# Dense expert weights built in steps of eight tokens, with the weighted one-hots on ScalarE

## Chip, cores and metric

One core of a Trainium2 chip. The metric is the device time of one execution in microseconds (us); the kernel before is given as the median of three runs.

## What is computed

A transformer block on 512 tokens (plus 16 meta tokens) of width 1024: a gated linear recurrence, an attention branch, and then a layer of 16,384 small experts, of which each token takes 128 (16 of each of 8 heads). The part that matters here is that layer:

```python
idx = jnp.take_along_axis(cidx, sel, axis=-1)
g = jax.nn.softmax(ts, axis=-1)
act = jax.nn.gelu(jnp.einsum('chkd,cd->chk', u[idx], xt))
coef = (g * act.astype(jnp.float32)).astype(xt.dtype)
return jnp.einsum('chk,chkd->cd', coef, v[idx])
```

`u` and `v` are the two expert tables. `idx` and `g` are, for each token, the 128 chosen experts and their softmax weights.

## The kernel before

The tokens are four chunks of 128. For three of them the experts are not gathered: the whole tables are multiplied, in 128 blocks of 128 experts. For a block, a first product gives gelu(x . u) as [expert, token] (function `first_dense`, float32r parts, lines 181 to 183 and the activation at line 820), this is multiplied by a dense table of softmax weights that is zero for experts that were not chosen, and a second product with v gives the output. The fourth chunk gathers its rows by index.

The dense table of a chunk is made by `scatter` (line 843), once for each of the three chunks, and goes to DRAM (`gd`) in four pieces of 32 tokens. An expert index is split into its block (upper bits) and its place in the block (lower bits). For each token, one 128x128 product adds up its 128 choices: the left operand `hot` is the one-hot of the place, the right operand `wj` the one-hot of the block times the softmax weight, and the outcome is [place, block].

The work goes in groups of four tokens, 96 groups in all:

- line 868, VectorE: `hb`, the one-hots of the blocks of four tokens in bf16, laid out [choice, block, token], the token innermost;
- line 870, VectorE: `hot`, the one-hots of the places, float32, [choice, token, place];
- lines 873 to 877: the weighted one-hot `wj` of each token, 128 elements, read out of `hb` in steps of four bf16 elements (8 bytes). ScalarE makes three of four (line 875, its scale is a column of `gt_`), VectorE the fourth (line 877);
- line 878, TensorE: four products in float32, into one PSUM bank of the ring `mm2` (three banks). Each appears as two matmul records, so 768 records for 384 products;
- line 879, ScalarE: the eviction of the bank's 512 columns into the staging tile `stg`, [place, block, token] with 32 tokens. It reads PSUM in order and writes one float32 every 32, that is, every 128 bytes.

`stg` has one buffer. After eight groups it is sent to DRAM by SyncE's queue (line 881). `hb`, `hot` and `wj` have two buffers each, in a pool `sp_` that is closed after the stage.

Three generators run in step (`interleave`, line 890): `scatter` of one chunk, `choose` of the next chunk (VectorE for the most part), and `first_ahead` (line 830), first products of expert blocks ahead of time, with their weight loads (line 166) and splits on ScalarE (line 155) and VectorE (line 156). Within an engine the order is not the program's: a scheduler orders the instructions by a model of their times, and each engine then runs its queue in that order. Only in the stretch after (`dense`, line 958, from 966 us on) is VectorE held to the program's order. There `stage` (line 939) loads the dense table and splits v into `vh` and `vl`, two buffers each of 4 KB a partition, in a pool `vp` that is open from before the dense-weight stage. 40 blocks of the first product are made before that stretch, however long the stage takes.

Of the kernel before, what the change touches and what calls it, by code (L numbers as in the profile page):

```python
# [8 lines left out]
F32 = mybir.dt.float32  # L9
# [12 lines left out]
NK = 8            # 128-row pieces of D_MODEL  # L22
NM = 16           # meta tokens
# [4 lines left out]
NH = 16           # attention heads  # L28
SCALE = 96.0 ** -0.5
PH = 8            # PEER heads  # L30
TOPK = 16
NS = PH * TOPK    # chosen experts of a token
NCAND = 50        # pairs (a, b) of ranks with (a + 1) * (b + 1) <= 16
NEG = -3.0e38
BIG = 1.0e30
# The pair of rank k (from 0) has (a + 1) * (b + 1) <= k + 1: blocks (a0, na, b0, nb) of pairs, by the
# group of four ranks that they can first have.
# [5 lines left out]
CO = (3, 0, 2, 1)    # chunks of queries of a pair of heads: the two sizes of the probabilities in turn  # L43
NJ = 128          # blocks of 128 experts
LAG = 41          # blocks that the first product runs ahead of the second
TS = 32           # tokens of a piece of the dense weights
JG = 4            # blocks of a load of the dense weights
# How the experts of a chunk are computed. Chunk 0: rows of both tables fetched by index.
# Chunks 1 to 3: products with both whole tables, times the dense softmax weights.
NDC = 3  # L50
ORD = (mybir.EngineType.DVE,)
SCA = 3           # tokens of four that ScalarE scales
LT = 2            # blocks of the first product between the two phases
GE = 6            # steps by which the fetches of rows end early
GA = ((0, 2), (2, 5))          # gate tiles that are computed between those of the recurrent branch
# [3 lines left out]
DT = NDC * P      # tokens of the dense chunks  # L59

# columns of the packed per-feature vectors
# [7 lines left out]
class in_order:  # L69
    """Keeps the instructions of the given engines that are traced within in the order of the program."""  # L70
# [22 lines left out]
def now(gen):  # L93
    """Runs a generator through; what it returns."""
    while True:
        try:
            next(gen)
        except StopIteration as e:
            return e.value
# [7 lines left out]
def interleave(*gens):  # L107
    """Runs generators in step, by the share of each that is done."""
    items = [[g, n, 0] for g, n in gens if n]
    while items:  # L110
        it = min(items, key=lambda i: i[2] / i[1])
        try:
            it[2] += next(it[0]) or 1
        except StopIteration:
            items.remove(it)
# [3 lines left out]
def hybrid_block_kernel(ctx: ExitStack, tc, hT, x, win, wkr, vecs, wgate, wrnn, watt, wuq, wukv, wout,  # L119
# [38 lines left out]
    wn = [0, 0, None]         # pieces, more buffers of the parts and their pool  # L158

    def wload(src, n, name):  # L160
        """A weight tile of n columns: its two float32r parts, in pieces of 512 columns."""
# [28 lines left out]
    # K' of a head: 64 rows without position, then the rotated rows twice  # L190
# [12 lines left out]
    def bcast_rms(sq, pieces, dim, dst, name):  # L203
        """dst = sqrt(mean of squares + eps) of every token (column), on all partitions."""
        for t0, n in pieces:
            o = mm1(f"{name}_ss{t0}")
            for k, q in enumerate(sq):
                TE.matmul(o[:, :n], onesP, q[:, t0:t0 + n], start=k == 0, stop=k == len(sq) - 1)
            A.activation(dst[:, t0:t0 + n], o[:, :n], AF.Sqrt, bias=eps_t, scale=1.0 / dim)

    # The projections take h * g; their outcomes are scaled by the token's 1/rms.
# [6 lines left out]
    def proj_tile(wi, full, name, src=None, m=P, w=None):  # L218
        """One tile of w_in: PSUM pieces (first token, tokens, psum); full: with the meta tokens."""
# [22 lines left out]
    def two(tags, name):  # L242
        """Eight [P, T] pieces in the space of two tiles."""
# [56 lines left out]
    def latent_norms():  # L300
        """The rotated key rows of all buffers, the normed latent of keys and values, the queries' scales."""
# [17 lines left out]
    # 8 * log_sigmoid(lambda) = 8 * (min(l, 0) - log1p(exp(-|l|)));  # L319
    # log1p(z) = 2 * atanh(y), y = z / (2 + z) <= 1/3  # L320
# [11 lines left out]
    for d in (13, 11, 9, 7, 5, 3, 1):  # L332
# [8 lines left out]
          for k in range(NK)]                              # recurrent output  # L341
    def sig_tile(wi, name):
        """Sigmoid of a tile of w_in."""
# [10 lines left out]
    def out_rnn(m):  # L354
        """A tile of the recurrent branch's gated outcome."""
# [11 lines left out]
    for hb in range(NK // HB):  # L367
# [53 lines left out]
        # 1 - a^2 = -tanh(log a) * (1 + a^2)  # L421
# [39 lines left out]
    def fm_pieces(pl, name):  # L461
        """A feature-major operand: the two parts of each 128-feature piece."""
# [5 lines left out]
    # the meta tokens in one product: rows hi, hi, lo of the values by hi, lo, hi of the probabilities  # L468
# [8 lines left out]
    def att_pair(pr):  # L477
        """Keys and values of a pair of heads."""
# [19 lines left out]
        # values of the tokens of each chunk  # L498
# [9 lines left out]
    def att_query(pr, j, pair):  # L508
        """Queries of a head."""
# [9 lines left out]
    def att_scores(st):  # L519
# [7 lines left out]
        for (k0, n), sp in zip(pieces, sps):  # L527
            d0 = nk - P - k0         # the diagonal block
# [20 lines left out]
    def att_turn(st):  # L549
        """Probabilities with the keys on the partitions, in parts; those of both heads side by side."""  # L550
# [21 lines left out]
    def att_out(st):  # L572
        """[feature of the pair, query of each head]: a head's own half of the features counts."""
# [54 lines left out]
    xdp = pool(ctx, "xd", "right")  # L628
    mx_ = pool(mixx, "mix")
    # normed input of the experts, feature-major: the dense chunks, then chunk 0  # L630
# [32 lines left out]
    def dense_products(j, o, w=None):  # L663
        """x . u of expert block j for the dense chunks: [expert, token]."""
# [7 lines left out]
    def mixing():  # L672
        """Attention output, gated sum of the branches, residual, second norm."""
# [50 lines left out]
    def key_scores():  # L724
        """Scores of the expert keys, the 16 best of each half."""
# [31 lines left out]
    def choose(i, c):  # L757
        """The 16 best pairs of each head, their indices and softmax weights."""
# [64 lines left out]
    def first_dense(j, o, w=None):  # L823
        """gelu(x . u) of expert block j for the dense chunks: [expert, token]."""
# [15 lines left out]
    iota4 = sp_.tile([P, P, 4], BF16, name="iota4")  # L840
    V.tensor_copy(iota4, iota.unsqueeze(2).to_broadcast([P, P, 4]))

    def scatter(gi, val, ef):
        """Dense [expert in block, block, token] weights of a chunk, to DRAM: one-hot products of each token."""
# [17 lines left out]
        for q in range(P // TS):  # L862
            stg = sp_.tile([P, NJ, TS], F32, tag="stg", bufs=1, name=f"stg{gi}_{q}")
            for t4 in range(0, TS, 4):
                o = mm2(f"sc{gi}_{q}_{t4}")
                t0 = q * TS + t4
                hb = sp_.tile([P, P, 4], BF16, tag="hb", bufs=2, name=f"hb{gi}_{t0}")
                V.tensor_tensor(hb, iota4, blk[:, t0:t0 + 4].unsqueeze(1).to_broadcast([P, P, 4]), op=OP.is_equal)
                hot = sp_.tile([P, 4, P], F32, tag="hot", bufs=2, name=f"hot{gi}_{t0}")
                V.tensor_tensor(hot, iota.unsqueeze(1).to_broadcast([P, 4, P]),  # L870
                                it[:, t0:t0 + 4].unsqueeze(2).to_broadcast([P, 4, P]), op=OP.is_equal)
                wj = sp_.tile([P, 4, P], F32, tag="wj", bufs=2, name=f"wj{gi}_{t0}")
                for u in range(4):
                    if u < SCA:
                        A.activation(wj[:, u, :], hb[:, :, u], AF.Copy, scale=gt_[:, t0 + u:t0 + u + 1])  # L875
                    else:
                        V.tensor_scalar(wj[:, u, :], hb[:, :, u], gt_[:, t0 + u:t0 + u + 1], None, op0=OP.mult)
                    TE.matmul(o[:, u * P:(u + 1) * P], hot[:, u, :], wj[:, u, :], start=True, stop=True)  # L878
                A.copy(stg[:, :, t4:t4 + 4].rearrange("p j t -> p t j"), o.rearrange("p (t j) -> p t j", t=4))  # L879
                yield  # L880
            nc.sync.dma_start(gd[gi, q], stg)
# [24 lines left out]
    def first_by_index(c):  # L906
        """coef = softmax weight * gelu(u[idx] . x) of the chosen experts."""
# [31 lines left out]
    def stage(j):  # L939
        """Operands of step j: the parts of u of block j + LAG, of v and of the coefficients of block j."""  # L940
# [61 lines left out]
def _consts():  # L1002
    """Constants that depend on the shapes alone."""
# [22 lines left out]
def _layout(i):  # L1026
# [7 lines left out]
    def tiles(w):                      # [K, N] -> [N / 128][128 of K][K / 128 * 128 of N]  # L1034
# [17 lines left out]
    uq = np.concatenate([uq, uq[..., 80:96], uq[..., 64:80]], -1)               # 3, p, h, 128  # L1052
# [30 lines left out]
```

## Time and profile before

| | |
|---|---|
| runs | 1882.66, 1877.91, 1879.43 us; median 1879.43 |
| span of the profiled execution | 1876.3 us (the page gives no other time for it) |
| TensorE matmul busy | 1821.0 us, 97% |
| VectorE busy | 1470.3 us, 78% |
| ScalarE busy | 981.4 us, 52% |
| GpSimd busy | 356.4 us, 19% |
| dense-weight stage | 719 to 966 us, 247 us |

The shares are means over stages that have different limits; the stage of the change is some 13% of the span. A group's mean duration is longer than the distance of two such instructions that follow each other, since they overlap in part: the busy time of a group counts an overlap once.

### The profile page before, as it was taken

How to read it: one execution, taken by the hardware profiler on the slowest of the kernel's cores; microseconds unless marked ns; L12 is line 12 of the kernel's file. 1: busy time of each engine (PE TensorE's matmuls, PEld its weight loads, DVE VectorE, ACT ScalarE, POOL GpSimd, SP SyncE). 2: the span in 40 equal slices, each digit the busy share in tenths (PEclk: the TensorE clock that was granted, in tenths of full speed). 3: DMA queues.
4: the chain of work that ended last, by engine and by line, in shares of the span. 5: the costliest groups of instructions: out<-in, count | busy, mean ns of one | idle time of the engine just before them, and what ended most of it. 6: DMA issues, size and time to landing. Idle time of an engine off the chain costs nothing.

```text
span 1876.3 us, 28456 instructions
## 1 busy us (share of the span) xinstructions
PE 1821.0 (97%) x9731; PEld 1600.0 (85%) x9731; DVE 1470.3 (78%) x3280; ACT 981.4 (52%) x1915; POOL 356.4 (19%) x295
## 2 busy tenths in 40 slices
PE   8999999999999999999999999999999999999997
PEld 7888778877788888888899999998999999998886
DVE  7787677777546999898858788787887888887775
ACT  5778576766334337999963333333333333333343
POOL 0100000000100000000014344344444444443310
PEclk9999999999999999999999999999999999999999
DMA  5333212112733223454569999989998899988764
GB/s 162 92 101 104 74 54 66 62 55 85 241 113 129 85 85 130 144 194 158 189 225 348 321 318 340 326 300 322 324 334 313 304 331 321 343 309 280 266 223 152
DMA packets 181602, 390.34 MB, mean 208 GB/s; under 512 B 16593, under 2 KB 68305, under 8 KB 179921
## 3 DMA queue, kind: packets, MB, share of 16 engines
q1 hardware_dynamic: 141632, 245.97, 38.9%
q0 software_dynamic: 39536, 142.00, 21.8%
q8 instruction: 76, 1.25, 0.3%
q14 instruction: 70, 0.57, 0.1%
q10 hardware_dynamic: 288, 0.56, 0.1%
HBM read 353.44 MB, written 34.08 MB: 207 GB/s over the span
## 4 chain that ended last, share of the span: by engine, by line
PE 73%; ACT 10%; DMA 6%; DVE 6%; issue 3%; POOL 0%; DVEq 0%; ACTq 0%; SPq 0%; POOLq 0%
PE y L183 8%; PE y L182 8%; PE y L181 8%; PE a L183 7%; PE a L182 7%; PE a L181 7%; ACT stg L879 4%; PE q L181 2%; PE q L182 2%; PE wgr_ps L228 2%; PE q L183 2%; PE wga_ps L228 2%; PE wgn_ps L228 2%; PE sc L878 2%; ACT wj L875 2%
## 5 line engine op out<-in xcount | busy, mean ns | idle before, releaser
L183 PE MATMUL a<-xdh,ut_l 128*128 128x384 f32 x1024 | 346.3, 338 | 4.3 <-DVE ut_l L156 4.3
L181 PE MATMUL a<-xdh,ut_h 128*128 128x384 f32 x1024 | 348.1, 340 | 0.7 <-ACT act L820 0.5
L182 PE MATMUL a<-xdl,ut_h 128*128 128x384 f32 x1024 | 345.7, 338 | 0.3 <-DVE xdl L156 0.3
L155 ACT CAST ut_h<-ut_w 128x512 fp32r<-128x512 f32 x256 | 159.2, 622 | 330.3 <-DMA ut_w<-in_peer_uT_dram 281.7
L183 PE MATMUL y<-vh,cl 128*128 128x512 f32 x768 | 300.6, 391 | 0.0
L182 PE MATMUL y<-vl,ch 128*128 128x512 f32 x768 | 300.3, 391 | 0.0
L181 PE MATMUL y<-vh,ch 128*128 128x512 f32 x768 | 299.0, 389 | 1.3 <-ACT ch L155 1.3
L902 POOL DMA_INDIRECT u<-in_peer_u_dram,eidx x128 | 162.7, 1271 | 682.9 <-DMA gt<-gd 458.5
L902 POOL DMA_INDIRECT v<-in_peer_v_dram,eidx x128 | 175.2, 1369 | 262.6 <-DVE acc L922 233.6
L156 DVE TENSOR_TENSOR ut_l<-ut_w,ut_h 128x512 fp32r<-128x512 f32 x256 | 170.5, 686 | 52.2 <-ACT ut_h L155 51.7
L183 PEld LDWEIGHTS a<-xdh,ut_l 128*128 128x128 f32 x1024 | 193.0, 188 | 5.2 <-DVE ut_l L156 5.0
L181 PEld LDWEIGHTS a<-xdh,ut_h 128*128 128x128 f32 x1024 | 193.0, 188 | 4.7 <-ACT act L820 0.9
L182 PEld LDWEIGHTS a<-xdl,ut_h 128*128 128x128 f32 x1024 | 192.9, 188 | 3.9 <-DVE xdl L156 0.5
L156 DVE TENSOR_TENSOR vl<-vr,vh 128x1024 fp32r<-128x1024 f32 x128 | 157.6, 1232 | 40.6 <-ACT vh L155 40.4
L155 ACT CAST ch<-gt 128x384 fp32r<-128x384 f32 x128 | 65.7, 513 | 233.8 <-DVE gt L952 228.8
L922 DVE SCALAR_TENSOR_TENSOR acc<-v,coef,acc 128x1024 f32<-128x1024 f32 x128 | 164.1, 1282 | 11.3 <-DMA v<-in_peer_v_dram,eidx 9.2
L183 PEld LDWEIGHTS y<-vh,cl 128*128 128x128 f32 x768 | 144.1, 188 | 30.6 <-DVE cl L156 0.3
L181 PEld LDWEIGHTS y<-vh,ch 128*128 128x128 f32 x768 | 144.2, 188 | 30.0 <-ACT ch L155 2.1
L182 PEld LDWEIGHTS y<-vl,ch 128*128 128x128 f32 x768 | 144.1, 188 | 28.4
L913 DVE SCALAR_TENSOR_TENSOR jk<-u,xn 128x1024 bf16<-128x1024 f32 x128 | 156.5, 1222 | 14.7 <-DMA u<-in_peer_u_dram,eidx 12.2
L155 ACT CAST vh<-vr 128x1024 fp32r<-128x1024 f32 x128 | 133.7, 1045 | 31.7 <-PE y L183 26.9
L156 DVE TENSOR_TENSOR cl<-gt,ch 128x384 fp32r<-128x384 f32 x128 | 71.5, 559 | 80.9 <-ACT ch L155 80.9
(349 smaller groups left out, 3569.2 us busy)
## 6 DMA issues: line engine op xcount, KB each, us to landing
ut_w<-in_peer_uT_dram SPq DMA_DIRECT2D x256, 256.0 KB, 6.2
vr<-in_peer_v_dram SPq DMA_DIRECT2D x128, 512.0 KB, 6.4
gd<-stg SPq DMA_DIRECT2D x12, 2048.0 KB, 7.3
gt<-gd SPq DMA_DIRECT2D x96, 256.0 KB, 6.9
wq_w<-in_wq_dram SPq DMA_DIRECT2D x32, 256.0 KB, 2.7
wxr_w<-in_win_dram SPq DMA_DIRECT2D x16, 256.0 KB, 2.7
wgr_w<-in_win_dram SPq DMA_DIRECT2D x16, 256.0 KB, 2.8
wga_w<-in_win_dram SPq DMA_DIRECT2D x16, 256.0 KB, 2.6
```

Of the source, the lines that this page charges most:

```text
L155: A.copy(dst_hi, src)
L156: V.tensor_sub(dst_lo, src, r32(dst_hi))
L181: TE.matmul(o, lh, rh, start=first, stop=False)
L182: TE.matmul(o, lh, rl, start=False, stop=False)
L183: TE.matmul(o, ll, rh, start=False, stop=last)
L228: TE.matmul(o[:m, :n], lhs, rhs[:, k, t0:t0 + n], start=k == 0 and i == 0, stop=k == NK - 1 and i == 2)
L875: A.activation(wj[:, u, :], hb[:, :, u], AF.Copy, scale=gt_[:, t0 + u:t0 + u + 1])
L878: TE.matmul(o[:, u * P:(u + 1) * P], hot[:, u, :], wj[:, u, :], start=True, stop=True)
L879: A.copy(stg[:, :, t4:t4 + 4].rearrange("p j t -> p t j"), o.rearrange("p (t j) -> p t j", t=4))
L902: G.indirect_dma_start(out=t, out_offset=None, in_=src, in_offset=bass.IndirectOffsetOnAxis(ap=eidx[:, s:s + 1], axis=0))
L913: V.scalar_tensor_tensor(jk, t, 1.0, xn2, op0=OP.mult, op1=OP.mult, accum_out=coef[:, s:s + 1])
L922: V.scalar_tensor_tensor(acc, t, coef[:, s:s + 1], acc, op0=OP.mult, op1=OP.add)
```

## The change

A step is eight tokens (`SG`) in place of four, 48 steps in all.

- `hb` is [choice, block, 8 tokens], made by one VectorE instruction of 1024 elements, and `hot` one of 1024 elements. There are 48 of each in place of 96.
- All eight weighted one-hots are made by ScalarE, 384 in place of 288 in all; VectorE makes none. They are read out of `hb` in steps of eight bf16 elements (16 bytes).
- `hot` and `wj` lie in the buffers of `vh` and `vl` in the pool `vp`, and no longer in `sp_`.
- The products of a step are written after the one-hots of the next step. Of the two banks of a step, the first is of the ring `mm2`, the second of the three banks with tag "s".
- The eviction goes [block, token]: it writes runs of four tokens, 16 bytes every 128 bytes, and reads PSUM in steps of 128 columns (512 bytes) within a run. There are still 96 evictions of 512 columns.
- The DMAs of the stage stay twelve; each is issued after the second eviction of the fourth step of its piece.

Comments are taken out throughout as well. The core of the diff:

```diff
-SCA = 3
+SG = 8
...
-    iota4 = sp_.tile([P, P, 4], BF16, name="iota4")
-    V.tensor_copy(iota4, iota.unsqueeze(2).to_broadcast([P, P, 4]))
+    iota8 = sp_.tile([P, P, SG], BF16, name="iota8")
+    V.tensor_copy(iota8, iota.unsqueeze(2).to_broadcast([P, P, SG]))
 
     def scatter(gi, val, ef):
         ei = sp_.tile([P, 2, NS], I32, tag="ei", bufs=1, name=f"ei{gi}")
         V.tensor_copy(ei[:, 0, :], ef)
         V.tensor_scalar(ei[:, 1, :], ei[:, 0, :], P - 1, None, op0=OP.bitwise_and)
...
         gt_ = sp_.tile([P, P], F32, tag="gt", bufs=1, name=f"gt{gi}")
         A.copy(gt_, o[:, 2 * P:3 * P])
         yield
-        for q in range(P // TS):
-            stg = sp_.tile([P, NJ, TS], F32, tag="stg", bufs=1, name=f"stg{gi}_{q}")
-            for t4 in range(0, TS, 4):
-                o = mm2(f"sc{gi}_{q}_{t4}")
-                t0 = q * TS + t4
-                hb = sp_.tile([P, P, 4], BF16, tag="hb", bufs=2, name=f"hb{gi}_{t0}")
-                V.tensor_tensor(hb, iota4, blk[:, t0:t0 + 4].unsqueeze(1).to_broadcast([P, P, 4]), op=OP.is_equal)
-                hot = sp_.tile([P, 4, P], F32, tag="hot", bufs=2, name=f"hot{gi}_{t0}")
-                V.tensor_tensor(hot, iota.unsqueeze(1).to_broadcast([P, 4, P]),
-                                it[:, t0:t0 + 4].unsqueeze(2).to_broadcast([P, 4, P]), op=OP.is_equal)
-                wj = sp_.tile([P, 4, P], F32, tag="wj", bufs=2, name=f"wj{gi}_{t0}")
+        def products(t0, hot, wj, stg):
+            q, t8 = divmod(t0, TS)
+            for h in range(0, SG, 4):
+                o = ps.tile([P, 512], F32, tag="s", bufs=3, name=f"sc{gi}_{t0 + h}") if h else mm2(f"sc{gi}_{t0}")
                 for u in range(4):
-                    if u < SCA:
-                        A.activation(wj[:, u, :], hb[:, :, u], AF.Copy, scale=gt_[:, t0 + u:t0 + u + 1])
-                    else:
-                        V.tensor_scalar(wj[:, u, :], hb[:, :, u], gt_[:, t0 + u:t0 + u + 1], None, op0=OP.mult)
-                    TE.matmul(o[:, u * P:(u + 1) * P], hot[:, u, :], wj[:, u, :], start=True, stop=True)
-                A.copy(stg[:, :, t4:t4 + 4].rearrange("p j t -> p t j"), o.rearrange("p (t j) -> p t j", t=4))
-                yield
-            nc.sync.dma_start(gd[gi, q], stg)
+                    TE.matmul(o[:, u * P:(u + 1) * P], hot[:, h + u, :], wj[:, h + u, :], start=True, stop=True)
+                A.copy(stg[:, :, t8 + h:t8 + h + 4], o.rearrange("p (t j) -> p j t", t=4))
+            if t8 + SG == TS:
+                nc.sync.dma_start(gd[gi, q], stg)
+        last = None
+        for t0 in range(0, P, SG):
+            if t0 % TS == 0:
+                stg = sp_.tile([P, NJ, TS], F32, tag="stg", bufs=1, name=f"stg{gi}_{t0 // TS}")
+            hb = sp_.tile([P, P, SG], BF16, tag="hb", bufs=2, name=f"hb{gi}_{t0}")
+            V.tensor_tensor(hb, iota8, blk[:, t0:t0 + SG].unsqueeze(1).to_broadcast([P, P, SG]), op=OP.is_equal)
+            hot = r32(vp.tile([P, D], F32R, tag="vh", bufs=2, name=f"hot{gi}_{t0}")).rearrange("p (t e) -> p t e", t=SG)
+            V.tensor_tensor(hot, iota.unsqueeze(1).to_broadcast([P, SG, P]),
+                            it[:, t0:t0 + SG].unsqueeze(2).to_broadcast([P, SG, P]), op=OP.is_equal)
+            wj = r32(vp.tile([P, D], F32R, tag="vl", bufs=2, name=f"wj{gi}_{t0}")).rearrange("p (t e) -> p t e", t=SG)
+            for u in range(SG):
+                A.activation(wj[:, u, :], hb[:, :, u], AF.Copy, scale=gt_[:, t0 + u:t0 + u + 1])
+            yield
+            if last:
+                products(*last)
+            last = (t0, hot, wj, stg)
+            yield
+        products(*last)
```

## Rows read from the trace of the kernel before

**Rows 1.** Busy time in windows of the dense-weight stage, then of the stretch after it.
```profile
core 0: us, PE busy (x) PEld busy (x) DVE busy (x) ACT busy (x) POOL busy (x), PEclk, DMA share, GB/s
719.00:798.00 79.00, 73.02 (x476) 66.19 (x475) 70.59 (x230) 74.35 (x162) 0.00 (x0) 1.00 0.41 144
798.00:878.00 80.00, 74.84 (x487) 68.91 (x486) 72.97 (x253) 75.40 (x163) 0.00 (x0) 1.00 0.48 168
878.00:966.00 88.00, 81.11 (x542) 77.77 (x541) 70.19 (x202) 80.31 (x170) 0.00 (x0) 1.00 0.51 181
960.00:1860.00 900.00, 897.41 (x4445) 803.45 (x4444) 707.78 (x950) 333.86 (x533) 337.95 (x256) 1.00 0.89 306
```

**Rows 2.** Chain of waits inside 719 to 966 us, its shares by line.
```profile
by line: ACT stg L879 29.6%; PE sc L878 13.1%; ACT wj L875 13.0%; DMA gd<-stg 9.3%; PE a L182 5.9%; PE a L183 5.7%; PE a L181 5.7%; ACT ut_h L155 4.7%; issue 4.5%; ACT act L820 3.1%; ACT L820 1.0%; DVE hot L870 0.5%; DVE ut_l L156 0.5%; ACT
```

**Rows 3.** Waits inside 719 to 966 us: waiter, releaser, total us, times, longest.
```profile
PEld sc L878 <- ACT wj L875: 31.2, 48, 2.1
...
PE sc L878 <- ACT wj L875: 12.1, 23, 1.3
ACT ut_h L155 <- PE a L182: 6.8, 11, 1.1
ACT wj L875 <- DVE hb L868: 5.2, 8, 1.5
ACT stg L879 <- DMA gd<-stg: 3.0, 3, 1.7
```

**Rows 4.** ScalarE's groups inside 719 to 966 us: busy us, mean ns, idle before.
```profile
L879 ACT COPY stg<-sc 128x512 f32<-128x512 f32 x96 | 101.6, 1111 | 4.0 <-DMA gd<-stg 3.0 <-PE sc L878 0.6
L875 ACT ACTIVATE wj<-hb,gt 128x128 f32<-128x128 bf16 x288 | 98.2, 412 | 5.7 <-DVE hb L868 5.2
L155 ACT CAST ut_h<-ut_w 128x512 fp32r<-128x512 f32 x60 | 37.6, 629 | 7.0 <-PE a L182 6.8
```

**Rows 5.** ScalarE's groups over the whole span, four comparable shapes.
```profile
L747 ACT COPY scs<-sc 128x512 f32<-128x512 f32 x16 | 9.4, 588 | 0.9 <-PE sc L745 0.7
...
L155 ACT CAST hgh<-gr 128x512 fp32r<-128x512 f32 x8 | 4.9, 617 | 6.3 <-DVE gr L432 6.3
...
L290 ACT ACTIVATE cqh<-cq,vec 128x512 fp32r<-128x512 f32 x3 | 2.1, 710 | 0.0
...
L810 ACT ACTIVATE gate<-gate 128x128 f32<-128x128 f32 x4 | 1.2, 311 | 0.0
```

**Rows 6.** VectorE's groups inside 719 to 966 us.
```profile
L870 DVE TENSOR_TENSOR hot<-iota,it 128x512 f32<-128x512 f32 x96 | 65.7, 684 | 2.7 <-PE sc L878 2.1
...
L868 DVE TENSOR_TENSOR hb<-iota,blk 128x512 bf16<-128x512 bf16 x96 | 39.7, 418 | 14.6 <-ACT wj L875 13.2 <-ACT blk L856 1.4
L877 DVE TENSOR_SCALAR wj<-hb,gt 128x128 f32<-128x128 bf16 x96 | 26.8, 279 | 0.3 <-ACT gt L860 0.3
```

**Rows 7.** VectorE's groups over the whole span, larger tiles.
```profile
L913 DVE SCALAR_TENSOR_TENSOR jk<-u,xn 128x1024 bf16<-128x1024 f32 x128 | 156.5, 1222 | 14.7 <-DMA u<-in_peer_u_dram,eidx 12.2
...
L803 DVE TENSOR_TENSOR work<-sf,cand_pos 128x1600 bf16<-128x1600 bf16 x4 | 3.9, 984 | 0.0
...
L803 DVE TENSOR_TENSOR work<-sf,cand_pos 128x640 bf16<-128x640 bf16 x4 | 1.9, 482 | 0.0
```

**Rows 8.** TensorE's groups inside 719 to 966 us.
```profile
L878 PE MATMUL sc<-wj,hot 128*128 128x128 f32 x768 | 109.6, 285 | 17.8 <-ACT wj L875 12.1 <-DVE hot L870 1.8 <-DVE wj L877 1.3
L181 PE MATMUL a<-xdh,ut_h 128*128 128x384 f32 x243 | 85.4, 352 | 0.0
```

**Rows 9.** TensorE in order of time near 947 us: start, us, instruction.
```profile
946.78 0.33 PE L182 MATMUL a<-xdl,ut_h 128*128 128x384 f32 x1
...
946.96 0.33 PE L183 MATMUL a<-xdh,ut_l 128*128 128x384 f32 x1
...
947.13 1.95 PE L878 MATMUL sc<-wj,hot 128*128 128x128 f32 x16
```

**Rows 10.** DMA issues of the page: the staging tile, KB each, us to landing.
```profile
gd<-stg SPq DMA_DIRECT2D x12, 2048.0 KB, 7.3
```

## Prediction

> **What bounds the kernel now.** Read the busy time in windows first [rows 1]. After 960 us TensorE is busy for 897.4 of 900 us with work that the change leaves alone, and 40 expert blocks of the first product are made before that stretch whatever the stage before it does. So the stretch only moves, and what the change is worth is the length of the stage from 719 to 966 us: 79 + 80 + 88 = 247 us. In it the reader should see three engines near their ends: ScalarE busy for 74.35 + 75.40 + 80.31 = 230.1 us, TensorE for 229.0, VectorE for 213.8. ScalarE idles for 16.9 us.
>
> The chain of waits of this stage runs over the evictions (29.6%) and the weighted one-hots (13.0%), both ScalarE's, before anything else [rows 2]. The waits say the same: TensorE waits for the one-hots (31.2 us at its weight loads, 12.1 of it as idle matmul time), while ScalarE's own waits are short [rows 3]. ScalarE bounds the stage, TensorE is close behind it.
>
> **The change, part by part.**
>
> *Evictions.* There are 96 before and after, of 512 columns. One takes 1111 ns [rows 4]; a ScalarE copy of the same shape out of PSUM that writes in order takes 588 [rows 5]. The difference, 523 ns or 1.02 ns an element, is what writing one element every 128 bytes costs. The new eviction writes four neighbours at a time but reads PSUM in steps of 512 bytes, and no row shows such a read. Bounds: it is free, and 96 x 523 ns = 50.2 us of ScalarE go; or it costs what the stepped write did, and nothing goes. I take the first: the row that prices a step is a write to SBUF, and nothing shows it for PSUM.
>
> *One-hots moved to ScalarE.* 96 more at 98.2 / 288 = 0.341 us of busy time each [rows 4]: +32.7 us on ScalarE, and 26.8 less on VectorE [rows 6].
>
> *The step of reading them.* All 384 now read `hb` in steps of 16 bytes, before 8. At 8 bytes the step is as good as free: an activation of 128 elements takes 311 ns, a scale out of a tile adds 710 - 617 = 93, together 404 [rows 5], and the one-hot takes 412 [rows 4]. Bounds: free again, 0 us; or the surcharge of the stepped write, 384 x 128 x 1.02 ns = 50.2 us (the number of elements is that of the evictions, so it is the same sum). Less than nothing is excluded, as 412 is already the unstepped time.
>
> The two rows lie on either side. I take the upper end, for this reason: an element in order costs (617 - 311) / 384 = 0.80 ns [rows 5], the stepped write 0.80 + 1.02 = 1.82 for each lone element. If memory gives a place at that pace, and two elements 8 bytes apart share a place, each costs 0.91 ns and 128 of them 14 ns more than in order: 8 are seen. Doubling the step then leaves each alone. That is an inference from two rows, no measurement, and it carries much of my doubt.
>
> [...]
>
> *VectorE.* `hb` of 1024 elements: 482 + 384 x (984 - 482) / 960 = 683 ns [rows 7], 48 times, 32.8 against 39.7 us. `hot` of 1024: some 1222 ns as for a float32 operation of that size [rows 7], 58.7 against 65.7. With the one-hots that moved, VectorE has 41 us less. That shortens nothing by itself; it removes ScalarE's waits for `hb` (5.2 us [rows 3]).
>
> *Products a step behind.* TensorE's matmuls are the same in number. Its waits for one-hots turn into slack where ScalarE keeps up, and come back at the next step where it does not. The float32 products run at 1.95 / 16 = 0.122 us, the first products at 0.17 [rows 9]: 768 x 0.122 + 3 x 243 x 0.173 = 220 us is about the least TensorE needs, 229 what it is busy for [rows 1, 8].
>
> *Buffers.* `hot` and `wj` in v's buffers cost nothing: v's first split comes after the stage, when the last products have read them. Should it be late, three blocks of first products (3 x 24 x 0.173 = 12 us) cover it.
>
> *The DMA of a piece.* Twelve, 7.3 us to landing [rows 10], out of one buffer. The next piece's eviction must wait for it, and on ScalarE's queue whatever stands behind the eviction waits too, for TensorE in the end. So far 3.0 us were lost to it [rows 3], since other work was put between. With a step of one-hots in between (8 x 0.34 to 0.47 us) I keep 3.0; were nothing else put there, it would be up to 12 x (7.3 - 2.7) = 55 us. SyncE's queue has the weight loads behind the DMA; their number and place change little, and the stage shows no wait for them.
>
> **The sum.** ScalarE: 230.1 - 50.2 + 32.7 + 50.2 = 262.8 us. Of its 16.9 us of idle time, those for `hb` (5.2) go, and those for TensorE's first products (6.8) mostly, since TensorE is then the one with slack; some 6 stay. The stage takes 269 us, 22 more. The span goes from 1876.3 to 1898; the median of the runs, 3.1 us above that span, from 1879.4 to **1901.4**. With 0 to 17 us of idle time the case reaches from 1895 to 1912. The same sum comes out if it is the PSUM read that costs the surcharge and the 16-byte step that doesn't. A difference under 0.3%, 5.6 us, can't be told from none here.
>
> **Rivals.**
>
> *Both steps are free* (faster). ScalarE falls to 230.1 - 50.2 + 32.7 = 212.6 us, under TensorE, which then sets the stage: 229 us of busy time with 0 to 11 of waits, or down to 224 if longer runs of products save switches: 224 to 240, some 13 us less, about 1866. For it: the 8-byte row, the one nearest in step and the same instruction. It turns where both steps together cost 0.58 ns an element: ScalarE then needs 212.6 + 49,152 x 0.58 ns = 241 us, and with 6 of idle time the stage is again 247; below that the change is faster.
>
> *Both steps cost the surcharge* (slower by far). ScalarE: 230.1 + 32.7 + 50.2 = 313 us, stage some 319, about 1951. For it: the only stepped access that is slow in this trace reads PSUM and writes SBUF, so it can't say which memory is the finicky one; against it, that every reader of PSUM in this trace is as fast as one of SBUF (588 against 617 [rows 5]).
>
> *Nothing to be told.* The queue order comes from a scheduler that knows none of these surcharges. It already runs 16 product records together [rows 9], so the products are partly a step behind now, and the change may do there nothing that it says. With one surcharge half as large (25 us), ScalarE needs 238 us and the stage some 244 to 250: within 0.3%.
>
> **How the numbers follow.** Forecast 0.44 (either surcharge alone); both free 0.32; both costly 0.14; nothing to be told 0.10. Faster by over 0.3% is most of the first rival, 0.30; the same 0.10; slower the rest, 0.60. The range takes in the forecast's case, the first rival and the middle, and leaves out the second rival: 1861 to 1915.
>
> **What would show it.** In the changed profile: the eviction near 588 ns (1111: the PSUM read costs); the one-hot near 412 + 131 = 543 ns (412: the 16-byte step is free); `hb` near 683 and `hot` near 1222; ScalarE's busy time over 95% of the stage, TensorE's waits for one-hots still the longest. The forecast is wrong if the one-hot stays at 412 with the eviction at 588: then TensorE's idle time in the stage is nearly gone.

## The result and the profile after

1895.45 us against 1878.78 (medians): the ratio is 1.0081, with a 95% interval of 1.0059 to 1.0102. The change made the kernel slower, by 17 us or so.

The profiled execution has a span of 1893.3 us, 17.0 over that of before. Where the 17 us lie is read from the windows, the dense-weight stage first, then the stretch after it:

```profile
core 0: us, PE busy (x) PEld busy (x) DVE busy (x) ACT busy (x) POOL busy (x), PEclk, DMA share, GB/s
722.00:802.00 80.00, 73.75 (x458) 66.30 (x457) 69.73 (x254) 78.99 (x183) 0.00 (x0) 1.00 0.39 139
802.00:890.00 88.00, 78.90 (x492) 70.77 (x490) 74.31 (x183) 87.89 (x196) 0.00 (x0) 1.00 0.44 159
890.00:984.00 94.00, 87.36 (x572) 83.51 (x573) 45.12 (x57) 93.97 (x214) 0.00 (x0) 1.00 0.48 169
...
977.00:1877.00 900.00, 895.02 (x4421) 800.29 (x4422) 707.07 (x948) 336.59 (x538) 334.44 (x256) 1.00 0.89 306
```

The stage now takes 80 + 88 + 94 = 262 us, where it took 247 [rows 1]: 15 of the 17 us. ScalarE is busy for 78.99 + 87.89 + 93.97 = 260.9 of them, all but 1.1 us; it was busy for 230.1 of 247. TensorE is busy for 240.0 of 262, with nearly the same products (1522 matmul records against 1505). The stretch after it is as full as before. The stage begins 3.3 us later than before, since the products of the expert queries (ahead of the key scores) begin at 580.0 in place of 576.7 us. What comes before them is not touched; in the other eight profiles of this block's kernels that point lies between 572.9 and 576.7, five of them of kernels made from the changed one, so I take it for scatter.

ScalarE's groups in the stage (busy us, mean ns of one, idle before), to be held against [rows 4]:

```profile
L886 ACT ACTIVATE wj<-hb,gt 128x128 f32<-128x128 bf16 x384 | 167.6, 568 | 0.8 <-ACT gt L860 0.8
L870 ACT COPY stg<-sc 128x512 f32<-128x512 f32 x96 | 51.7, 617 | 0.0
```

The eviction went from 1111 to 617 ns, and its group from 101.6 to 51.7 us of busy time. The weighted one-hot went from 412 to 568 ns, and its group from 98.2 to 167.6 us. What the eviction gave, the one-hots took, and 20 us more. ScalarE's own total grew by 30.8 (260.9 - 230.1): of the other 11 us, 2.1 are v's first two casts, which now fall into the stage, and 8 come from groups that overlap each other less than before (25.7 us in place of 33.5, the sum of all groups less the total).

VectorE's two remaining one-hots, to be held against [rows 6]:

```profile
L882 DVE TENSOR_TENSOR hot<-iota,it 128x1024 f32<-128x1024 f32 x48 | 58.2, 1220 | 0.7 <-PE sc L869 0.6
...
L879 DVE TENSOR_TENSOR hb<-iota,blk 128x1024 bf16<-128x1024 bf16 x48 | 33.2, 691 | 48.3 <-ACT wj L886 42.5 <-ACT blk L856 5.7
```

Together 91.4 us in place of 132.2: the third group is gone (26.8), and the other two take 14.0 less. But VectorE did not bound the stage, and now it waits for ScalarE. The waits of the stage, to be held against [rows 3]:

```profile
DVE hb L879 <- ACT wj L886: 42.5, 30, 3.6
...
PE sc L869 <- ACT wj L886: 7.1, 9, 1.5
...
PE a L181 <- ACT ut_h L155: 5.6, 5, 2.0
...
PE a L183 <- DVE ut_l L156: 3.3, 7, 1.3
PE sc L869 <- ACT stg L870: 3.1, 3, 2.2
```

All of them end at ScalarE, or at what VectorE makes of ScalarE's casts. TensorE now waits for the one-hots (7.1 us) less than before (12.1), but also for the casts of its own first products, directly (5.6) and over VectorE (3.3), and for evictions (3.1). ScalarE waits for next to nobody. The chain of waits of the stage says the same in one line; 54.0% is the one-hots, where 13.0% was [rows 2]:

```profile
by line: ACT wj L886 54.0%; ACT stg L870 15.2%; ACT ut_h L155 9.7%; issue 4.7%; ACT act L820 4.3%; DMA gd<-stg 2.9%; ACT L810 1.5%; ACT L820 1.0%; DVE ut_l L156 0.9%; DVE hot L882 0.8%; DVE hb L879 0.8%; PE a L183 0.7%; DVE sel L791 0.7%; P
```

### The profile page after: what moved, and what is told of

The parts are those of the page before. It is cut to its first block, busy times and chain, and to the rows that moved or that the text cites. A ratio compares the mean times of both kernels' runs of the same rounds, so it can differ in the third digit from the quotient of the medians.

```text
span 1893.3 us, 28323 instructions
## 1 busy us (share of the span) xinstructions
PE 1830.0 (97%) x9731; PEld 1603.8 (85%) x9731; DVE 1445.9 (76%) x3088; ACT 1010.2 (53%) x2011; POOL 352.8 (19%) x295
## 4 chain that ended last, share of the span: by engine, by line
PE 45%; issue 18%; ACT 16%; DMA 8%; DVE 7%; POOL 6%; DVEq 0%; POOLq 0%; ACTq 0%; SPq 0%
ACT wj L886 7%; PE y L181 4%; PE y L183 4%; PE y L182 4%; POOL v L913 4%; DMA v<-in_peer_v_dram,eidx 3%; PE a L183 2%; PE a L182 2%; PE a L181 2%; PE q L181 2%; POOL u L913 2%; ACT stg L870 2%; PE q L182 2%; PE wgr_ps L228 2%; PE q L183 2%
## 5 line engine op out<-in xcount | busy, mean ns | idle before, releaser
L183 PEld LDWEIGHTS a<-xdh,ut_l 128*128 128x128 f32 x1024 | 192.8, 188 | 12.5 <-DVE ut_l L156 12.3
L886 ACT ACTIVATE wj<-hb,gt 128x128 f32<-128x128 bf16 x384 | 167.6, 568 | 0.8 <-ACT gt L860 0.8
```

What stands on the lines that cost most here:

```text
L183: TE.matmul(o, ll, rh, start=False, stop=last)
```

## Experiments

Ratios are to the kernel before, run beside each kernel on the same chip, with their 95% intervals. The kernel before took 1882.49 us beside the first four and 1886.00 beside the others, so a time of the one group is held against a time of the other by its ratio. Where a stage is given, it goes from the first one-hots to the last eviction.

### The 8-byte step back

```diff
-hb = sp_.tile([P, P, SG], BF16, tag="hb", ...)
+hb = sp_.tile([P, 2, P, 4], BF16, tag="hb", ...)
...
-    A.activation(wj[:, u, :], hb[:, :, u], AF.Copy, ...)
+    A.activation(wj[:, u, :], hb[:, u // 4, :, u % 4], AF.Copy, ...)
```

`hb` is still one VectorE instruction of 1024 elements; only its layout differs.

> The one-hots of a step lie in two halves of four tokens, so that ScalarE reads them in steps of 8 bytes again; all else as in the changed kernel. Theory (the 16-byte step is the cost): a weighted one-hot takes 412 ns as before in place of 568, ScalarE loses 384 x 0.095 = 37 us of its 261 in the stage and is at 224, TensorE then sets the stage at 229 to 240 us in place of 262, and the time is 1862 to 1873 us, under the kernel before. Rival (it is the 96 more one-hots on ScalarE and the coarser steps, whatever the layout): the one-hot stays over 540 ns or the time stays within 4 us of 1895.

Measured: 1863.52 us, ratio 0.9909 (0.9889 to 0.9930). ScalarE's one-hots and the window of the stage:

```profile
L886 ACT ACTIVATE wj<-hb,gt 128x128 f32<-128x128 bf16 x384 | 121.7, 412 | 3.4 <-PE sc L869 1.6 <-DVE hb L879 1.0 <-ACT gt L860 0.8
```

```profile
715.00:944.00 229.00, 219.32 (x1505) 215.33 (x1504) 186.98 (x492) 217.64 (x590) 0.00 (x0) 0.99 0.48 178
```

The one-hot is back at 412 ns, to the nanosecond what it was, with the same number on ScalarE as in the changed kernel. ScalarE's busy time falls from 260.9 to 217.6 us: 43.2 us were the price of the step alone, 43.2 / 384 = 113 ns a one-hot or 0.88 ns an element. The stage takes 229 us. The rival falls: neither the number of the one-hots nor the coarser steps made the kernel slower, the layout did.

### The old eviction in the changed kernel

```diff
-A.copy(stg[:, :, t8 + h:t8 + h + 4], o.rearrange("p (t j) -> p j t", t=4))
+A.copy(stg[:, :, t8 + h:t8 + h + 4].rearrange("p j t -> p t j"), o.rearrange("p (t j) -> p t j", t=4))
```

> The eviction of the kernel before (reads PSUM in order, writes every 128 bytes) in the changed kernel. Theory (ScalarE alone sets the stage, and the new eviction gave back 50 us of it): 1111 ns an eviction, ScalarE 311 us, the stage 311 to 316, the time 1944 to 1950 us. Rival (part of ScalarE's work is covered, or the new eviction's gain was small): under 25 us slower than the changed kernel.

Measured: 1935.84 us, ratio 1.0279 (1.0254 to 1.0305), 40 us over the changed kernel, between the theory's 50 and the rival's 25.

```profile
L886 ACT ACTIVATE wj<-hb,gt 128x128 f32<-128x128 bf16 x384 | 165.6, 533 | 0.8 <-ACT gt L860 0.8
L870 ACT COPY stg<-sc 128x512 f32<-128x512 f32 x96 | 94.3, 1106 | 0.0
```

```profile
719.00:1018.00 299.00, 258.69 (x1514) 237.42 (x1514) 189.64 (x491) 297.86 (x588) 0.00 (x0) 0.93 0.37 136
```

ScalarE is busy for 297.9 of 299 us, so it sets the stage, as the theory has it. The size was off because it came from mean durations. The group's busy time, in which overlaps count once, is 94.3 against 51.7 us, 42.6 more; ScalarE's total grows by 37.0 us and the stage by 37 (262 to 299). That is less than the 40 us of the time: what follows the stage takes 916 us here and 909 in the changed kernel, while the stage begins 3 us earlier. The granted clock is 0.93 in the stage, where TensorE is busy for 258.7 of 299 us, and 0.98 from 1025 to 1125 us; it is 1.00 in the changed kernel, in its stage and in the 100 us from 990 on. A one-hot also takes a little less here than in the changed kernel (533 against 568 ns).

### The new eviction alone, in the kernel before

```diff
-A.copy(stg[:, :, t4:t4 + 4].rearrange("p j t -> p t j"), o.rearrange("p (t j) -> p t j", t=4))
+A.copy(stg[:, :, t4:t4 + 4], o.rearrange("p (t j) -> p j t", t=4))
```

> The new eviction alone, in the kernel before: groups of four tokens, a quarter of the one-hots on VectorE, products in the same group. Theory: an eviction takes some 610 ns, ScalarE falls from 230 to 180 us, TensorE sets the stage at 229 to 240 us, the time is 1862 to 1872 us. Rival (TensorE's waits for one-hots come from the order, not from ScalarE's load, and need the products a step behind): the time stays within 5 us of 1879.

Measured: 1857.01 us, ratio 0.9869 (0.9846 to 0.9892).

```profile
L875 ACT ACTIVATE wj<-hb,gt 128x128 f32<-128x128 bf16 x288 | 98.4, 406 | 6.8 <-DVE hb L868 6.2 <-PE sc L878 0.2
L879 ACT COPY stg<-sc 128x512 f32<-128x512 f32 x96 | 54.1, 588 | 9.6 <-PE sc L878 6.3 <-DMA gd<-stg 2.8
```

```profile
PE sc L878 <- ACT wj L875: 2.6, 4, 1.4
```

```profile
718.00:940.00 222.00, 218.89 (x1497) 211.37 (x1497) 210.07 (x683) 193.80 (x492) 0.00 (x0) 1.00 0.51 183
```

One line of the change, by itself, makes the kernel 1.3% faster, and no kernel below is faster than this one beyond the intervals. An eviction takes 588 ns, just what the copy in order out of PSUM took [rows 5]. The stage is 222 us long, with TensorE busy for 218.9: TensorE sets it. It came out under the 229 that was expected as the lower end, since TensorE's busy time fell as well, from 229.0 to 218.9 us with about as many records (1505 and 1497); why it was longer before is not shown. The 220 us worked out from the pace of its products [rows 9] was the better floor. TensorE waits 2.6 us for one-hots in place of 12.1 [rows 3], with the products in the same group, so most of that wait did come from ScalarE's load.

### A quarter of the one-hots back on VectorE

```diff
-A.activation(wj[:, u, :], hb[:, :, u], AF.Copy, scale=gt_[:, t0 + u:t0 + u + 1])
+if u % 4 != 3:
+    A.activation(wj[:, u, :], hb[:, :, u], AF.Copy, scale=gt_[:, t0 + u:t0 + u + 1])
+else:
+    V.tensor_scalar(wj[:, u, :], hb[:, :, u], gt_[:, t0 + u:t0 + u + 1], None, op0=OP.mult)
```

> Every fourth weighted one-hot back on VectorE, all else as in the changed kernel, the step of 16 bytes too. Theory (ScalarE's load sets the stage): ScalarE loses 96 x 0.436 = 42 us and is at 219, VectorE gains some 27 and is near 216, TensorE sets the stage at 229 to 245 us, the time is 1862 to 1878 us, with the one-hots of ScalarE still near 550 ns. Rival (VectorE pays as much for the 16-byte step, so that it becomes the bound or holds up ScalarE): its one-hot takes well over 279 ns, and the time stays over 1885 us.

Measured: 1869.86 us, ratio 0.9936 (0.9916 to 0.9956), in the theory's range.

```profile
L889 DVE TENSOR_SCALAR wj<-hb,gt 128x128 f32<-128x128 bf16 x96 | 27.6, 329 | 0.0
```

```profile
718.00:949.00 231.00, 220.78 (x1506) 217.27 (x1506) 208.33 (x587) 221.46 (x493) 0.00 (x0) 0.99 0.49 177
```

VectorE pays for the 16-byte step too, 329 ns against 279 [rows 6], as the rival has it, but the time is not over the rival's 1885. With ScalarE at 221.5 us and TensorE at 220.8 the stage takes 231 us. So the change can be mended from either end, by the layout or by the share: what was wrong was ScalarE's sum.

### The access by itself

A kernel that leaves the whole block out and holds only groups of eight equal instructions, one form a line. The order on ScalarE's queue is the scheduler's again: it mixed most of the groups, instruction by instruction, with others that use other tiles. Only the float32 reads from 8 bytes on, and VectorE's groups, ran one group after the other.

> The access itself: none of the block is computed, only groups of eight equal ScalarE and VectorE instructions, 128 elements each (512 out of PSUM), one form a line; its time says nothing. Theory (memory gives places of 16 bytes, and an access that finds one element in each pays a fixed surcharge): bf16 reads at 2, 4 and 8 bytes take the same time, 12 bytes somewhat more, 16, 32 and 128 bytes the same surcharge of 0.7 to 1.0 ns an element; float32 reads at 16 bytes and more and float32 writes at 16 bytes and more pay it too, at 8 bytes not; reads of PSUM at 512 bytes pay nothing (about 590 ns for 512 elements). Rival (the cost grows with the step): 32 and 128 bytes cost clearly more than 16.

ScalarE, 128 elements, its scale out of a tile. In this order: bf16 reads at 2, 4, 8, 12, 16, 32 and 128 bytes (lines 39 to 45), float32 reads at 8, 12, 16, 32 and 128 bytes (48 to 52), float32 writes at 8, 16 and 128 bytes (54 to 56), both at 128 bytes (58). 512 elements out of PSUM: in order (60), read at 512 bytes and written in order (61) or in runs of four (62), read in order and written at 128 bytes (63). The view lists them by cost, without the float32 reads:

```profile
L63 ACT COPY big<-pt 128x512 f32<-128x512 f32 x8 | 8.4, 1051 | 0.0
L62 ACT COPY big<-pt 128x512 f32<-128x512 f32 x8 | 5.0, 625 | 0.0
...
L60 ACT COPY flat<-pt 128x512 f32<-128x512 f32 x8 | 4.8, 594 | 1.4 <-PE pt L36 1.4
L45 ACT ACTIVATE dst<-bf,sc 128x128 f32<-128x128 bf16 x8 | 4.5, 567 | 0.0
...
L58 ACT ACTIVATE ds<-ff,sc 128x128 f32<-128x128 f32 x8 | 4.4, 550 | 0.0
L55 ACT ACTIVATE ds<-ff,sc 128x128 f32<-128x128 f32 x8 | 4.3, 543 | 0.0
L43 ACT ACTIVATE dst<-bf,sc 128x128 f32<-128x128 bf16 x8 | 4.3, 532 | 0.0
...
L42 ACT ACTIVATE dst<-bf,sc 128x128 f32<-128x128 bf16 x8 | 3.7, 467 | 0.0
...
L54 ACT ACTIVATE ds<-ff,sc 128x128 f32<-128x128 f32 x8 | 3.6, 454 | 0.0
...
L41 ACT ACTIVATE dst<-bf,sc 128x128 f32<-128x128 bf16 x8 | 3.5, 439 | 0.0
L39 ACT ACTIVATE dst<-bf,sc 128x128 f32<-128x128 bf16 x8 | 3.4, 421 | 1.7 <-DVE sc L27 1.7
```

The float32 reads, in the order in which they ran (shortest, middle and longest of the eight in ns, then the first and the last start in us):

```profile
L48 ACT ACTIVATE dst<-ff,sc x8: 406/406/442, 55.4 to 58.5; 128x128 f32<-128x128 f32 x8
...
L49 ACT ACTIVATE dst<-ff,sc x8: 461/464/469, 58.9 to 62.4; 128x128 f32<-128x128 f32 x8
...
L50 ACT ACTIVATE dst<-ff,sc x8: 522/525/527, 62.9 to 66.8; 128x128 f32<-128x128 f32 x8
...
L51 ACT ACTIVATE dst<-ff,sc x8: 521/532/534, 67.4 to 71.3; 128x128 f32<-128x128 f32 x8
...
L52 ACT ACTIVATE dst<-ff,sc x8: 507/507/508, 71.9 to 75.6; 128x128 f32<-128x128 f32 x8
```

The float32 reads show it best; the 8- and the 12-byte ones ran beside the same VectorE copies (line 70) but for the last of them. At 8, 12 and 16 bytes their means are 411, 464 and 525 ns, and no read of one group is as long as one of the next. So 12 bytes cost 53 ns more than 8, about half of the 114 that 16 bytes cost; 32 and 128 bytes cost no more than 16 (529 and 507). The bf16 reads, mixed with others, take 421, 465, 439 and 467 ns at 2, 4, 8 and 12 bytes, and 532, 551 and 567 at 16, 32 and 128. As 4 bytes come out 26 ns above 8, a mean of these mixed rows can be off by some 30 ns or more, so they show the cost at 16 bytes but can't tell whether 12 are free.

Writes cost 454 ns at 8 bytes, 543 and 531 at 16 and 128; read and written in order, 128 float32 take 446 (line 47, mixed with others too). So the cost sets in above 8 bytes, as the theory has it with "12 bytes somewhat more", is whole at 16 and does not grow with the step from there: the rival falls. A read and a write at 128 bytes together (550) cost hardly more than one of them (507 and 531).

PSUM read at 512 bytes costs 625 ns for 512 elements, written in order or in runs, against 594; even these 31 ns, 0.06 an element, are not clearly the step's, since the eight copies in order grew from 576 to 616 ns as they ran. The eviction of before costs 1051.

VectorE, bf16 reads at 2, 8, 16 and 32 bytes (65 to 68), and the new and the old eviction (70, 71):

```profile
L71 DVE COPY big<-pt 128x512 f32<-128x512 f32 x8 | 8.3, 1042 | 0.3
...
L70 DVE COPY big<-pt 128x512 f32<-128x512 f32 x8 | 5.5, 691 | 34.8 <-ACT big L63 34.6
...
L68 DVE TENSOR_SCALAR dst<-bf,sc 128x128 f32<-128x128 bf16 x8 | 2.7, 334 | 0.3
L67 DVE TENSOR_SCALAR dst<-bf,sc 128x128 f32<-128x128 bf16 x8 | 2.6, 331 | 0.3
L65 DVE TENSOR_SCALAR dst<-bf,sc 128x128 f32<-128x128 bf16 x8 | 2.3, 287 | 6.4 <-ACT dst L52 6.1
L66 DVE TENSOR_SCALAR dst<-bf,sc 128x128 f32<-128x128 bf16 x8 | 2.3, 286 | 0.3
```

The same here: 287 and 286 ns at 2 and 8 bytes, 331 and 334 at 16 and 32 (12 was not run); 691 against 1042 for the eviction.

### The products not a step behind

To the kernel with the 8-byte step:

```diff
-            if last:
-                products(*last)
-            last = (t0, hot, wj, stg)
-            yield
-        products(*last)
+            products(t0, hot, wj, stg)
+            yield
```

> The 8-byte step, and the products written in the step of their one-hots in place of a step behind; else as in the changed kernel. Theory (the order is the scheduler's, and with ScalarE no longer over-full the stage is TensorE's 220 us whatever the order in the program): within 5 us of the kernel with the 8-byte step alone (1863.5). Rival (the lag of a step is what keeps TensorE fed): TensorE's waits for one-hots come back, 5 to 15 us slower, 1869 to 1879.

Measured: 1858.80 us, ratio 0.9857 (0.9828 to 0.9886), against 0.9909 (0.9889 to 0.9930) with the lag; the intervals just part. The stage takes 225 us in place of 229:

```profile
717.00:942.00 225.00, 218.55 (x1501) 213.99 (x1500) 187.12 (x492) 218.66 (x590) 0.00 (x0) 1.00 0.50 181
```

Without the lag TensorE waits 1.2 us for one-hots in the stage, with it 2.0, so the rival falls: the lag keeps nothing fed that would not be fed without it. If it does anything it costs some 4 us by the stages, or 10 by the ratios. The two were not measured beside each other, so that much stays open.

### The 8-byte step and a quarter on VectorE

The two edits above together.

> The 8-byte step, and every fourth weighted one-hot back on VectorE. Theory: ScalarE goes from 218 to some 188 us in the stage, TensorE's 219 to 220 us are left as the only bound, the stage is 221 to 224 us in place of 229, the time 1856 to 1861 us, no better than the kernel before with the new eviction alone (1857.0). Rival (the steps of eight tokens are worth something of their own once ScalarE is relieved): under 1852 us.

Measured: 1856.73 us, ratio 0.9838 (0.9812 to 0.9864).

```profile
718.00:940.00 222.00, 217.39 (x1505) 216.29 (x1506) 204.32 (x589) 192.37 (x495) 0.00 (x0) 0.98 0.51 184
```

With ScalarE down to 192.4 us the stage takes 222, as long as with the new eviction alone, and the time can't be told from that. In these two kernels TensorE is busy for 217 to 219 of 222 us, so that a further relief of ScalarE or VectorE could give 3 to 5 us at most.

### v's buffers for the one-hots

```diff
-hot = sp_.tile([P, 4, P], F32, tag="hot", ...)
+hot = r32(vp.tile([P, D], F32R, tag="vh", ...)).rearrange("p (t e) -> p t e", e=P)[:, :4, :]
...
-wj = sp_.tile([P, 4, P], F32, tag="wj", ...)
+wj = r32(vp.tile([P, D], F32R, tag="vl", ...)).rearrange("p (t e) -> p t e", e=P)[:, :4, :]
```

This is made to the kernel before with the new eviction.

> The kernel before with the new eviction, and its one-hots put in v's buffers as the change does; groups of four and all else as before. Theory (this part costs something after all: v's first two blocks can no longer be split early, and stand before the first coefficients on ScalarE's queue): TensorE waits 1.4 to 3.5 us for the coefficients at the first second product, where the kernel without it waits 0; 1857.0 becomes 1858 to 1861. Rival (the wait has to do with the stage's own end): no such wait, the time within 1 us.

Measured: 1859.60 us, ratio 0.9856 (0.9829 to 0.9882): no difference from 0.9869 that can be told. The wait is there, but a small one. After the stage, first with v's buffers used, then in the changed kernel:

```profile
DVE gt L952 <- DMA gt<-gd: 5.8, 1, 5.8
...
ACT ch L155 <- DVE gt L952: 4.6, 2, 3.0
...
PEld y L181 <- ACT ch L155: 1.5, 1, 1.5
PE y L181 <- ACT ch L155: 1.2, 1, 1.2
```

```profile
DVE gt L963 <- DMA gt<-gd: 6.3, 1, 6.3
ACT ch L155 <- DVE gt L963: 4.7, 2, 3.4
...
PE y L181 <- ACT ch L155: 3.2, 1, 3.2
```

Without this part TensorE has no wait at its first second product. With it, it waits 1.2 us here (1.5 at the weight load) and 3.2 in the changed kernel. The wait ends at a chain: the last piece goes to DRAM, the coefficients come back from it, VectorE multiplies them, ScalarE casts them (`ch`). In all nine profiles the first second product starts 12.3 to 13.0 us after the last piece was issued, and TensorE waits where its first products run out before that. Here v's first cast stands between the last two evictions on ScalarE (start us, us, instruction):

```profile
937.59 0.59 ACT L879 COPY stg<-sc 128x512 f32<-128x512 f32 x1
938.07 1.05 ACT L155 CAST vh<-vr 128x1024 fp32r<-128x1024 f32 x1
939.02 0.59 ACT L879 COPY stg<-sc 128x512 f32<-128x512 f32 x1
```

The last products end at some 938.5 us, so the cast holds the last piece up by about 0.5 us. In the changed kernel it stands there too, from 981.5 us on, and the last eviction follows at 982.5; in the kernel before, v's first two casts come at 581 and 584 us, long ahead of their use. The theory, that they stand before the coefficients on ScalarE's queue, is not what the trace shows: right before `ch` ScalarE is idle, for 1.5 us here and 3.4 in the changed kernel, until VectorE's product is there, and that waits for the DMA of the coefficients (5.8 and 6.3 us). What the rest of the waits comes from stays open.

## Why the prediction was right, and where its terms were off

The forecast was 1901.4 us by one mechanism: the new eviction gives ScalarE 50 us, 96 more one-hots take 33, their wider step takes 50 back, and ScalarE, which bounds the stage, ends 33 us fuller. ScalarE's busy time went from 230.1 to 260.9 us, 30.8 more. The kernel with the 8-byte step shows the mechanism by itself, as it takes away the step and nothing else, and with it the whole loss.

*Evictions.* Right: 51.7 us of busy time, where 101.6 - 50.2 = 51.4 was the sum. Reading PSUM in steps is as good as free (617 ns an eviction, 588 for the copy in order [rows 5]), the end of the bounds that was taken.

*The 16-byte step.* The end that was chosen is the right one. It costs 43.2 us where 50.2 was the term; 0.88 ns an element where the stepped write had given 1.02. The picture behind it, two elements that share a place in memory and a fixed pace for each place, was the author's inference from two rows, and no run shows the places. What the runs show is the cost by step: for float32 reads 53 ns more at 12 bytes than at 8, 114 at 16, and 118 and 96 at 32 and 128.

*The one-hots moved.* 32.7 us was the term. The group of the kernel with the 8-byte step has 121.7 us for 384, 23.5 more than 98.2 for 288: an instruction takes 0.317 us of busy time in place of 0.341, and why is not shown. A group's sum does not see its overlap with other groups (25.7 us over all groups in the changed kernel, 33.5 before), so ScalarE's own total is the safer number. It came out at 260.9 us against 262.8, and that it is so near is in part luck: the step's term was 7.0 us too large, and all the rest together 5 too small.

*Idle time.* 6 us of ScalarE's idle time were to stay, and 1.1 stayed. With ScalarE's errors nearly cancelled, these 5 us are most of why the stage took 262 us, not 269, and the time was 1895.45 in place of 1901.4. ScalarE, where it bounds the stage, runs nearly without gaps here: 1.1 us idle of 262, and 1.1 of 299 with the old eviction.

*VectorE.* 691 and 1220 ns, where 683 and 1222 were worked out. That it would shorten nothing by itself was right.

*TensorE's waits.* "TensorE's waits for one-hots still the longest" holds for the single longest only: 7.1 us for one-hots stand beside 5.6 and 3.3, together 8.9, for the weights of the first products, which the prediction did not have. ScalarE makes the casts of the first products as well, and was late with these too.

*Buffers.* "Cost nothing" holds for the time as far as it can be told (0.9856 against 0.9869), but the step missed a wait of 1.2 us. It had v's first split after the stage; in the kernel before it comes at 581 us, and in the changed kernel between the last two evictions.

*The DMA of a piece.* Kept at 3.0 us; the changed kernel shows no such wait.

*The rivals.* The first rival's case, both steps free, is what the kernel with the 8-byte step shows: 229 us for the stage, within the rival's 224 to 240. The second, both steps costly, falls with the eviction at 617 ns, and in the access by itself at 625 against 594. The third, nothing to be told, falls with the interval (1.0059 to 1.0102).

## What to carry to other kernels

Look at the byte step of the innermost loop of every ScalarE and VectorE access, reads and writes of SBUF alike: here 8 bytes were as good as free (ScalarE's float32 reads and writes 411 and 454 ns, 446 in order; VectorE's bf16 reads 286 and 287), 12 cost ScalarE about half of the surcharge (53 of 114 ns), and from 16 on an element cost 0.3 to 1.0 ns more (45 ns for 128 on VectorE, 523 for 512 on ScalarE). A transposing eviction should take its step on PSUM's side (625 against 1051 ns on ScalarE, 691 against 1042 on VectorE), and a change of layout that saves work on one engine has to be costed on the engine that reads it. Where several edits come together, try the cheapest alone: here one line gave 1.3%, and the rest took it back.

## What was not expected of the hardware

- On ScalarE the cost of a step is about half there at 12 bytes and whole at 16, and then it does not grow: 411, 464, 525, 529 and 507 ns for float32 reads at 8, 12, 16, 32 and 128 bytes. VectorE pays too, 331 ns at 16 bytes against 286 at 8.
- Steps on both sides of one access do not add: 550 ns against 531 (write alone) and 507 (read alone).
- ScalarE and VectorE read PSUM in steps of 512 bytes at nearly full pace: 625 against 594 ns on ScalarE for 512 elements, 691 on VectorE, whose one-hots of that size, written in order, took 684 [rows 6].
